# Norm blocks turned into a pair of score banks instead of two single banks

## The chip, the cores and the metric

The kernel runs on one core of one Trainium2 chip. The metric is the device time of one execution in microseconds (us); the unchanged kernel takes 1291.82 us, the median of three runs (1291.59 to 1291.99). The core has five instruction queues that run side by side and wait for each other through semaphores: TensorE (PE: matmuls and transposes), VectorE (DVE), ScalarE (ACT), GpSimd (POOL), and SyncE (SP), which issues the transfers. Results of matmuls and transposes land in PSUM, which the kernel lays out in banks of 128 partitions by 512 numbers of 32 bits.

## The reference

One layer of a decoder: 16 learned tokens are put ahead of 1024 input tokens (1040 in all, 1024 features), the sum is normalized, projected into seven parts, given to two kinds of heads (differential attention and a gated recurrence), projected back, and followed by a convolutional feed-forward part. Only the first step and the projection behind it matter here:

```python
h = jnp.concatenate([meta, x], axis=1)          # 1040 x 1024
a = rmsnorm(h, ln_mix_pre[l])                   # x * rsqrt(mean(x*x) + EPS) * gain
proj = a @ w_in[l]
dq, dk, dv, hq, hf, hi, hg = jnp.split(proj, SPLITS, axis=-1)
```

## The kernel before

**The first norm.** The tokens are taken in nine blocks of 128 (the last has 16), counted from 0 here; the third, fifth, seventh and ninth are blocks 2, 4, 6 and 8. For each block ACT squares the row with a running sum (`pre_stat`; its output `pj` is a throw-away tile in PSUM, the sum is `ss`) and makes 1/rms of it with a logarithm and an exponential. DVE multiplies the row by 1/rms and by the gain, in two halves of 512 features (`pre_scale`, output `xs`). PE turns each half into four 128x128 transposes (`pre_turn`, output `px`, line 292). ACT then copies the half rounded to a shorter format (`pre_hi`, a CAST, `a<-px`), and DVE subtracts this copy from the original for the remainder (`pre_lo`, a TENSOR_TENSOR, also `a<-px,a`). In the rows with numbers, `a00`, `a01`, `a02` are the rounded parts of three groups of tokens (0 to 255, 256 to 639, 640 to 1039), and `a10`, `a11`, `a12` their remainders.

**The projections beside it.** A projection of one column tile is three matmuls for each of eight feature blocks: rounded weights with rounded activations, rounded weights with the remainder, and remainder of the weights with rounded activations. Those of the first head of attention (`pi_dq`, `pi_dk`, `pi_dv` for query, key, value) run between the transposes of the norm blocks: the first group of tokens during blocks 2 to 4, the second during blocks 5 to 8. When a projection of a group is done, ACT and DVE take it out of PSUM (`q`, `k`, `kl` and `vt` in the rows), and its bank can be used again: `pi_dv` of the first group takes the bank of `pi_dq`. The weights `w3` of `pi_dv` are rounded on DVE (a CAST, `w<-wr_dv`) and their remainder is made on POOL.

**PSUM banks.** The pool has three kinds of tiles, each with two buffers: `ps_in` (one bank, projections), `ps_m` (one bank, everything small), and `ps_s` (a pair of banks, `[P, 2, 512]`, later the attention scores, in the norm the throw-away `pj`). A half block `px` takes a `ps_m` bank. Block 1 alone already takes one `ps_s` pair for both its halves (`spare`).

**What sets the order.** PE's order is written out: `interleave` runs the projections and the norm blocks as generators and mixes them by a cost budget. On ACT, DVE, POOL and SP a scheduler orders the instructions when the program is built, by its own estimates, and it puts in every semaphore wait. It keeps a record of who read and wrote each tile: a writer waits for the readers of what it overwrites, and a tile that gets a used buffer waits for the users of the tile before. Each engine runs its own list strictly in order, so that a wait holds everything behind it.

Of the kernel before, what the change touches and what calls it, by code (L numbers as in the profile page):

```python
# [90 lines left out]
def layer_kernel(ctx: ExitStack, tc: tile.TileContext, x, meta, table, lbl, gpre, gpost, win,  # L91
# [60 lines left out]
    def ps_m(name):  # L152
        return pp.tile([P, 512], F32, tag="m", name=name)

    def ps_s(name):
        return pp.tile([P, 2, 512], F32, tag="S", name=name)
# [115 lines left out]
    def pre_rows(i):  # L272
        return min(P, L - P * i)

    def pre_stat(i):
        r = pre_rows(i)
        junk = ps_s(f"pj{i}").rearrange("p a c -> p (a c)")
        ss = zp.tile([P, 1], F32, tag="ss", name=f"ss{i}", bufs=3)
        A.activation(junk[:r], xts[i][:r], AF.Square, accum_out=ss[:r])
        rstd_of(ss[:r], ss[:r], D)  # L280
        return ss

    def pre_scale(i, half, ss, xs):
        r = pre_rows(i)
        cs = slice(512 * half, 512 * half + 512)
        V.scalar_tensor_tensor(xs[:r, :512], xts[i][:r, cs], ss[:r], gb[:r, cs], ALU.mult, ALU.mult)

    def pre_turn(i, half, xs, pt=None):
        r = pre_rows(i)
        pt = ps_m(f"px{i}_{half}") if pt is None else pt  # L290
        for j in range(4):
            T.transpose(pt[:, j * r:(j + 1) * r], xs[:r, P * j: P * (j + 1)], ident[:r, :r])
        pv = pt[:, : 4 * r].rearrange("p (k t) -> p k t", k=4)
        return pv, slice(4 * half, 4 * half + 4), slice(P * i, P * i + r)

    def pre_hi(pv, ks, s):
        return A.copy(act(0, ks, s.start, s.stop), pv)

    def pre_lo(pv, ks, s):
        return V.tensor_tensor(act(1, ks, s.start, s.stop), pv, act(0, ks, s.start, s.stop).bitcast(F32), op=ALU.subtract)  # L300

    def pre_block(i):
        if i in stat:
            ss = stat[i]
        else:
            with tc.issue_after(last_hi.ins):
                ss = pre_stat(i)
        if i in xts:
            xs = zp.tile([P, D], F32, tag="xs", name=f"xs{i}")
            for half in range(2):  # L310
                pre_scale(i, half, ss, xs[:, 512 * half:])
            xts.pop(i)
        else:
            xs = xss[i, 0]
        for half in range(2):
            out_ = pre_turn(i, half, xs[:, 512 * half:])
            pre_hi(*out_)
            turned[i] = pre_lo(*out_)
            yield
# [614 lines left out]
    def pre_blocks(bs):  # L934
        for i in bs:
            yield from pre_block(i)
            if i + 4 < NBLK:
                load_x(i + 4)
# [865 lines left out]
```

## Time and profile before

| | |
|---|---|
| median of three runs | 1291.82 us |
| the profiled execution | 1290.12 us |
| its span, first to last instruction | 1288.3 us |
| PE busy in the span | 1268.2 us (98%) |
| DVE, ACT, POOL busy | 904.2, 692.1, 409.4 us |
| mean granted TensorE clock | 0.997 of full |
| the norm's transposes (`px`) | first at 7.8, last at 44.3 us from the start |

The profile is of one execution. A timeline row gives start and length in us, the engine, the line of the kernel, the operation, out<-in, the shapes and, after x, how many instructions were merged; in brackets stands how long the engine was idle just before and what ended it. L57 is the wrapper through which all DVE and ACT work goes, so these are told apart by their tiles. A window row gives for a stretch the busy time of each engine with its number of instructions, then the granted clock, the share of the DMA engines and GB/s. Matmuls overlap: a matmul's length is longer than the time until the next one starts.

### The profile page before, as it was taken

What the parts mean: (1) busy time and instruction counts of PE and PEld (TensorE: products, weight loads), DVE (VectorE), ACT (ScalarE), POOL (GpSimd) and SP (SyncE); (2) the same over time, 40 slices, a digit from 0 to 9 for tenths busy, and PEclk for the clock granted to TensorE, in tenths of its full rate; (3) what the DMA queues carried; (4) which work ended last, traced back from release to release, by engine and by line L of the source; (5) the groups of instructions that cost most, each with busy time, mean ns of one, the idle gap of its engine ahead of it and who ended that gap; (6) DMA issues with size and microseconds to landing.
All of it is one profiled execution on the core that took longest, in us unless ns stands there. A gap on an engine that the chain in (4) does not pass through costs nothing.

```text
span 1288.3 us, 26390 instructions
## 1 busy us (share of the span) xinstructions
PE 1268.2 (98%) x10264; PEld 1181.5 (92%) x10264; DVE 904.2 (70%) x1579; ACT 692.1 (54%) x1698; POOL 409.4 (32%) x322
## 2 busy tenths in 40 slices
PE   7999999999999999999999999999999999999997
PEld 7899999999999999777999999999999998888886
DVE  6576647564757476747797778778778786697587
ACT  7465357545654566446665445445445454454454
POOL 3221212021212110122165766766766730010120
PEclk9999999999999999999999999999999999999999
DMA  6222222212222223837512322222222237955363
GB/s 223 95 84 69 84 83 98 70 68 83 99 73 89 66 91 110 269 104 241 204 59 84 112 77 91 75 83 90 76 83 85 81 101 233 340 185 172 90 213 123
DMA packets 84387, 153.07 MB, mean 119 GB/s; under 512 B 9587, under 2 KB 19859, under 8 KB 84262
## 3 DMA queue, kind: packets, MB, share of 16 engines
q1 hardware_dynamic: 84262, 151.39, 35.4%
q8 instruction: 80, 1.31, 0.4%
q14 instruction: 45, 0.37, 0.1%
HBM read 112.69 MB, written 38.67 MB: 117 GB/s over the span
## 4 chain that ended last, share of the span: by engine, by line
PE 66%; DVE 2%; ACT 1%; DMA 0%; issue 0%; DVEq 0%
PE pd L1616 5%; PE pd L1615 5%; PE pd L1614 5%; PE pb L1415 4%; PE pb L1416 4%; PE pb L1417 4%; PE pa L1416 3%; PE pa L1417 3%; PE pa L1415 3%; PE pc L1416 3%; PE pc L1415 3%; PE pc L1417 3%; PE py L1030 2%; PE py L1034 2%; PE py L1032 2%; PE pq L1392 2%
## 5 line engine op out<-in xcount | busy, mean ns | idle before, releaser
L1415 PE MATMUL pb<-t,uh 128*128 128x258 f32 (+1 forms) x456 | 127.4, 279 | 0.6 <-DVE u L57 0.6
L1416 PE MATMUL pb<-t,uh 128*128 128x258 f32 (+1 forms) x456 | 127.3, 279 | 0.0
L1417 PE MATMUL pb<-t,ul 128*128 128x258 f32 (+1 forms) x456 | 127.2, 279 | 0.0
L1616 PE MATMUL pd<-wh,gl 128*128 128x512 f32 (+1 forms) x314 | 121.0, 386 | 0.0
L1615 PE MATMUL pd<-wl,gh 128*128 128x512 f32 (+1 forms) x314 | 120.5, 384 | 0.4 <-DVE wl L57 0.3
L1614 PE MATMUL pd<-wh,gh 128*128 128x512 f32 (+1 forms) x314 | 120.8, 385 | 0.0
L57 DVE SCALAR_TENSOR_TENSOR c<-uu,cwt,c 128x512 f32<-128x512 f32 x88 | 94.9, 1079 | 22.2 <-ACT c L57 21.4
L1364 POOL TENSOR_TENSOR c<-c,c 128x512 f32<-128x512 f32 x44 | 64.3, 1462 | 127.1 <-ACT c L57 112.9
L57 DVE SCALAR_TENSOR_TENSOR c<-ug,cwt,c 128x512 f32<-128x512 f32 x88 | 83.9, 954 | 6.6 <-ACT c L57 5.9
L1415 PEld LDWEIGHTS pb<-t,uh 128*128 128x128 f32 x456 | 85.8, 188 | 0.9 <-DVE u L57 0.8
L1416 PEld LDWEIGHTS pb<-t,uh 128*128 128x128 f32 x456 | 85.9, 188 | 0.0
L1417 PEld LDWEIGHTS pb<-t,ul 128*128 128x128 f32 x456 | 85.9, 188 | 0.0
L1416 PE MATMUL pa<-t,uh 128*128 128x256 f32 (+1 forms) x304 | 85.3, 281 | 0.0
L1417 PE MATMUL pa<-t,ul 128*128 128x256 f32 (+1 forms) x304 | 85.2, 280 | 0.0
L1415 PE MATMUL pa<-t,uh 128*128 128x256 f32 (+1 forms) x304 | 85.2, 280 | 0.0
L1417 PE MATMUL pc<-t,ul 128*128 128x256 f32 x304 | 83.9, 276 | 0.0
L1415 PE MATMUL pc<-t,uh 128*128 128x256 f32 x304 | 83.9, 276 | 0.0
L1416 PE MATMUL pc<-t,uh 128*128 128x256 f32 x304 | 83.9, 276 | 0.0
L1615 PEld LDWEIGHTS pd<-wl,gh 128*128 128x128 f32 x314 | 58.9, 188 | 14.0 <-DVE wl L57 1.5
L1616 PEld LDWEIGHTS pd<-wh,gl 128*128 128x128 f32 x314 | 59.0, 188 | 12.1
L1614 PEld LDWEIGHTS pd<-wh,gh 128*128 128x128 f32 x314 | 59.0, 188 | 11.6
L57 ACT ACTIVATE c<-ug,cbt,cwt 128x512 f32<-128x512 f32 x44 | 35.9, 817 | 44.0 <-issue 26.2
(421 smaller groups left out, 4278.2 us busy)
## 6 DMA issues: line engine op xcount, KB each, us to landing
ra<-in_wup_dram SPq DMA_DIRECT2D x76, 256.0 KB, 2.7
wd<-in_wdown_dram SPq DMA_DIRECT2D x44, 256.0 KB, 3.3
tsc<-wd SPq DMA_DIRECT2D x44, 256.0 KB, 2.5
gsc<-c SPq DMA_DIRECT2D x44, 256.0 KB, 2.0
wi<-tsc SPq DMA_DIRECT2D x44, 256.0 KB, 2.9
gi<-gsc SPq DMA_DIRECT2D x33, 256.0 KB, 4.0
wi<-in_wdown_dram SPq DMA_DIRECT2D x33, 256.0 KB, 3.7
msc<-mm SPq DMA_DIRECT2D x21, 256.0 KB, 3.6
```

The costliest lines, as they stand in the source:

```text
L57: ins = call(*args, **kw)
L1030: T.matmul(py[:r], mh[:, j, :r], hi, start=(first and j == 0), stop=False)
L1032: T.matmul(py[:r], mh[:, j, :r], lo, start=False, stop=False)
L1034: T.matmul(py[:r], ml[:, j, :r], hi, start=False, stop=(last and k == k1 - 1))
L1364: G.tensor_tensor(cg, cg, cu, op=ALU.mult)
L1392: T.matmul(pt, hi[:, s], th[:, k], start=(kh + k == 0), stop=False)
L1415: T.matmul(pt, hi[:, s], th[:, k], start=(first and k == 0), stop=False, skip_group_check=True)
L1416: T.matmul(pt, hi[:, s], tl[:, k], start=False, stop=False, skip_group_check=True)
L1417: T.matmul(pt, lo[:, s], th[:, k], start=False, stop=(k == 3), skip_group_check=True)
L1614: T.matmul(py, gh[:, s], wh, start=(k == 0 and pr not in (3, 7)), stop=False, skip_group_check=True)
L1615: T.matmul(py, gh[:, s], wl, start=False, stop=False, skip_group_check=True)
L1616: T.matmul(py, gl[:, s], wh, start=False, stop=(k == NH - 1), skip_group_check=True)
```

## The change

Blocks 2, 4, 6 and 8 take one `ps_s` pair for both halves, as block 1 does, instead of two `ps_m` banks. Blocks 3, 5 and 7 keep theirs. The number of operations, their shapes and PE's order stay the same.

```diff
         for half in range(2):
-            out_ = pre_turn(i, half, xs[:, 512 * half:])
+            if i % 2 == 0 and half == 0:
+                pair = ps_s(f"px{i}")
+            out_ = pre_turn(i, half, xs[:, 512 * half:], None if i % 2 else pair[:, half])
             pre_hi(*out_)
             turned[i] = pre_lo(*out_)
             yield
```

The rows below are the built programs' instructions in order, with the semaphores that each waits for. PE before, from the middle of the first group's projections: `px2_0` and `px2_1` are the two halves of block 2, `px3_0` the first half of block 3.

```order
L896 MATMUL pi_dk0_0_163<-a00_105,wl_dk0_1_272 128x256 [waits Pool_49]
L896 MATMUL pi_dk0_0_163<-a00_105,wl_dk0_1_272 128x256
L292 MATMUL px2_1_324<-ident_73,xs2_267 128x128 [waits DVE_49,PE_49]
L292 MATMUL px2_1_324<-ident_73,xs2_267 128x128 x3
L896 MATMUL pi_dk0_0_163<-a00_105,wl_dk0_1_272 128x256 x2
L896 MATMUL pi_dq0_0_162<-a10_106,wh_dq0_1_240 128x256 x4
L896 MATMUL pi_dk0_0_163<-a10_106,wh_dk0_1_271 128x256
L292 MATMUL px3_0_347<-ident_73,xs3_344 128x128 [waits DVE_49]
L292 MATMUL px3_0_347<-ident_73,xs3_344 128x128 x3
L896 MATMUL pi_dk0_0_163<-a10_106,wh_dk0_1_271 128x256 x3
L249 MATMUL pi_dv0_0_363<-a00_105,w30_281 128x256 [waits DVE_49,PE_49]
```

And PE with the change, where `px2` is the pair of block 2, and the row shown with it is the second half:

```order
L898 MATMUL pi_dk0_0_163<-a00_105,wl_dk0_1_272 128x256 [waits Pool_49]
L898 MATMUL pi_dk0_0_163<-a00_105,wl_dk0_1_272 128x256
L292 MATMUL px2_310<-ident_73,xs2_267 128x128 [waits DVE_49]
L292 MATMUL px2_310<-ident_73,xs2_267 128x128 x3
L898 MATMUL pi_dk0_0_163<-a00_105,wl_dk0_1_272 128x256 x2
L898 MATMUL pi_dq0_0_162<-a10_106,wh_dq0_1_240 128x256 x4
L898 MATMUL pi_dk0_0_163<-a10_106,wh_dk0_1_271 128x256
L292 MATMUL px3_0_346<-ident_73,xs3_343 128x128 x4
L898 MATMUL pi_dk0_0_163<-a10_106,wh_dk0_1_271 128x256 x3
L249 MATMUL pi_dv0_0_362<-a00_105,w30_281 128x256 [waits DVE_49,PE_49]
```

The second half of block 2 and the first half of block 3 have exchanged their waits. Before, `px2_1` waits for its input `xs2` and for an old bank; its count on DVE is that of the second half of `xs2`. `px3_0` gets the bank of `px2_0` and waits on DVE until that is free, which is after the subtraction `a11<-px2_0`. With the change `px3_0` has an old bank and no wait of its own, and the second half of `px2` waits on DVE for a higher count than before: the subtraction of the first half, which reads the same tile. The same holds for `px4`, `px6` and `px8`.

DVE before, from the first weights' rounding on:

```order
L57 CAST w30_281<-wr_dv0_0_235 128x512 [waits DMAHW4_49]
L57 SCALAR_TENSOR_TENSOR xs3_344<-xt3_219,ss3_276,gb_122 128x512
L57 CAST w31_282<-wr_dv0_1_244 128x512 [waits DMAHW5_49]
L57 TENSOR_TENSOR a11_109<-px2_0_310,a01_108 128x4x128 [waits Activation_49]
L57 TENSOR_TENSOR a11_109<-px2_1_324,a01_108 128x4x128 [waits Activation_49]
L57 SCALAR_TENSOR_TENSOR q0_0_133<-pi_dq0_0_162,q0_0_133 64x256 [waits PE_49,Activation_49]
L57 SCALAR_TENSOR_TENSOR q1_0_134<-pi_dq0_0_162,q1_0_134 64x256
L57 SCALAR_TENSOR_TENSOR xs4_389<-xt4_222,ss4_385,gb_122 128x512 [waits DMAHW3_49,DVE_49,Activation_49]
L57 TENSOR_TENSOR a11_109<-px3_0_347,a01_108 128x4x128 [waits Activation_49]
```

and with the change:

```order
L57 CAST w30_281<-wr_dv0_0_235 128x512 [waits DMAHW4_49]
L57 SCALAR_TENSOR_TENSOR xs3_343<-xt3_219,ss3_276,gb_122 128x512
L57 CAST w31_282<-wr_dv0_1_244 128x512 [waits DMAHW5_49]
L57 TENSOR_TENSOR a11_109<-px2_310,a01_108 128x4x128 [waits Activation_49]
L57 SCALAR_TENSOR_TENSOR xs4_388<-xt4_222,ss4_384,gb_122 128x512 [waits DVE_49,DMAHW3_49,PE_49,Activation_49]
L57 TENSOR_TENSOR a11_109<-px2_310,a01_108 128x4x128 [waits Activation_49]
L57 SCALAR_TENSOR_TENSOR xs4_388<-xt4_222,ss4_384,gb_122 128x512
L57 SCALAR_TENSOR_TENSOR q0_0_133<-pi_dq0_0_162,q0_0_133 64x256 [waits PE_49,Activation_49]
L57 SCALAR_TENSOR_TENSOR q1_0_134<-pi_dq0_0_162,q1_0_134 64x256
L57 TENSOR_TENSOR a11_109<-px3_0_346,a01_108 128x4x128 [waits Activation_49]
```

The list is the same up to the subtraction of block 2's first half. Behind it the scale `xs4` of block 4 has moved ahead of the second half's subtraction and of the query's two subtractions `q0`, `q1`, and its first row now waits for PE, since it overwrites `xs2` while the second half of `px2` still has to be turned.

ACT before, from the query's copies to the second half of block 4:

```order
L57 ACTIVATE q0_0_133<-pi_dq0_0_162 64x256 [waits PE_49]
L57 ACTIVATE q1_0_134<-pi_dq0_0_162 64x256
L57 ACTIVATE ss4_385<-ss4_385 128x1 [waits Activation_49]
L57 ACTIVATE pj5_459,ss5_460<-xt5_246 128x1024 [waits DMAHW6_49,DVE_49]
L57 CAST a01_108<-px3_0_347 128x4x128 [waits PE_49]
L57 CAST k0_0_135<-pi_dk0_0_163 64x256 [waits PE_49]
L57 CAST k0_0_135<-pi_dk0_0_163 64x256
L57 CAST k1_0_136<-pi_dk0_0_163 64x256 x2
L57 CAST a01_108<-px3_1_368 128x4x128 [waits PE_49]
L57 ACTIVATE ss5_460<-ss5_460,eps_78 128x1 [waits Activation_49]
L57 ACTIVATE pj6_506,ss6_507<-xt6_342 128x1024 [waits DMAHW7_49,DVE_49]
L57 CAST a01_108<-px4_0_392 128x4x128 [waits PE_49]
```

and with the change:

```order
L57 ACTIVATE q0_0_133<-pi_dq0_0_162 64x256 [waits PE_49]
L57 ACTIVATE q1_0_134<-pi_dq0_0_162 64x256
L57 CAST a01_108<-px3_0_346 128x4x128 [waits PE_49]
L57 CAST k0_0_135<-pi_dk0_0_163 64x256 [waits PE_49]
L57 CAST k0_0_135<-pi_dk0_0_163 64x256
L57 CAST k1_0_136<-pi_dk0_0_163 64x256 x2
L57 CAST a01_108<-px3_1_367 128x4x128 [waits PE_49]
L57 ACTIVATE pj5_457,ss5_458<-xt5_246 128x1024 [waits DMAHW6_49,DVE_49]
L57 CAST a01_108<-px4_391 128x4x128 [waits PE_49]
L57 ACTIVATE ss5_458<-ss5_458,eps_78 128x1 [waits Activation_49]
L57 ACTIVATE pj6_504,ss6_505<-xt6_341 128x1024 [waits DMAHW7_49]
L57 ACTIVATE ss5_458<-ss5_458 128x1 [waits Activation_49]
```

The sum `pj5` of block 5 has moved behind the key's copies and block 3, directly ahead of block 4's first half, and the copy of a second half now also waits for the subtraction of the first. Some way behind, `pj7` and `pj8` move in the same way, to either side of the first half of block 6. From the third group's projections on, all lists are the same.

## The prediction

> **What bounds the kernel now.** The page's first part and the window view first: where does PE, the busiest engine, stand still?
>
> ```profile
> PE 1268.2 (98%) x10264; PEld 1181.5 (92%) x10264; DVE 904.2 (70%) x1579; ACT 692.1 (54%) x1698; POOL 409.4 (32%) x322
> ...
> 48.00:200.00 152.00, 150.62 (x1392) 142.78 (x1392) 87.76 (x209) 81.14 (x241) 30.18 (x32) 1.00 0.28 89
> 200.00:600.00 400.00, 396.39 (x3734) 364.86 (x3733) 250.14 (x569) 221.04 (x656) 73.00 (x70) 1.00 0.33 109
> 600.00:1000.00 400.00, 398.69 (x3329) 393.10 (x3329) 316.53 (x412) 216.79 (x441) 238.02 (x163) 1.00 0.29 98
> 1000.00:1255.00 255.00, 254.73 (x1410) 220.94 (x1409) 192.46 (x290) 127.05 (x250) 52.06 (x37) 1.00 0.54 178
> ```
>
> PE is busy in 98% of the span. From 48 to 1255 us, stretches of 152 + 400 + 400 + 255 = 1207 us, it is busy for 150.62 + 396.39 + 398.69 + 254.73 = 1200.43, so it stands for 6.6 us, and its granted clock is 1.00. Whatever delays PE before 48 us has at most these 6.6 us to be made up in. The changed stage lies wholly before 48 us, so I read that stretch as a timeline, its first stall first.
>
> ```profile
> 17.08 0.63 PE L292 MATMUL px<-ident,xs 128*128 128x128 f32 x4
> ...
> 17.78 0.64 PE L896 MATMUL pi_dq<-a,wh_dq 128*128 128x256 f32 x4
> ...
> 18.25 0.28 PE L896 MATMUL pi_dk<-a,wh_dk 128*128 128x256 f32 x1
> ...
> 18.78 1.05 ACT L57 CAST a<-px 128x512 fp32r<-128x512 f32 x2
> ...
> 19.37 1.48 DVE L57 CAST w<-wr_dv 128x512 fp32r<-128x512 f32 x1
> ...
> 20.78 1.27 DVE L57 TENSOR_TENSOR a<-px,a 128x512 fp32r<-128x512 f32 x2
> ...
> 21.51 0.82 PE L292 MATMUL px<-ident,xs 128*128 128x128 f32 x4 [2.98 <-DVE a L57]
> ...
> 21.99 0.99 PE L896 MATMUL pi_dk<-a,wh_dk 128*128 128x256 f32 x3
> 22.07 0.86 DVE L57 SCALAR_TENSOR_TENSOR q<-pi_dq,q 64x256 fp32r<-64x256 f32 x2
> ...
> 23.07 0.55 PE L249 MATMUL pi_dv<-a,w 128*128 128x256 f32 x1
> ...
> 23.42 0.42 PE L251 MATMUL pi_dv<-a,w 128*128 128x256 f32 x1
> ...
> 23.64 0.41 PE L253 MATMUL pi_dv<-a,w 128*128 128x256 f32 x1
> ```
>
> The transposes at 17.08 are the second half of block 2, those at 21.51 the first half of block 3. Between them PE runs eleven issues, has nothing left at 18.25 + 0.28 = 18.53, and stands for 2.98 us, until DVE has subtracted block 2's first half. This subtraction is the first of the two at 20.78, so it ends at about 20.78 + 1.27/2 + 0.04 = 21.46. It is late for nothing that PE or ACT owes it: ACT's two copies are over at 18.78 + 1.05 = 19.83. It stands in DVE's list behind the rounding of the second value weights, which runs from 19.37 to 20.85.
>
> ```profile
> 21.00:22.00 1.00, 0.49 (x5) 0.49 (x5) 1.00 (x2) 0.95 (x2) 1.00 (x1) 0.93 0.92 311
> ...
> 22.00:25.00 3.00, 2.90 (x14) 2.64 (x13) 2.91 (x6) 2.05 (x5) 0.22 (x1) 0.50 0.32 78
> ...
> 25.00:26.00 1.00, 1.00 (x9) 1.00 (x9) 0.95 (x4) 0.84 (x3) 0.00 (x0) 0.86 0.00 0
> ```
>
> The clock column (0.93, 0.50 and 0.86; windows of two views, by start) says that behind the stall TensorE runs at half clock: 0.07 of a microsecond lost is 0.14 us at half, so from 21.86, and to 25.28. In it matmuls of this size start 0.22 us apart (23.42, 23.64); the four at 17.78 took 18.25 - 17.78 = 0.47 until the next, 0.12 each.
>
> **The change part by part.** No operation is added or removed; four second halves get a wait, the banks of `px3`, `px5`, `px7` come free earlier, and DVE and ACT are reordered. I go through PE's list and write how far it runs behind the kernel before.
>
> *Block 2.* The second half now waits for the subtraction that ends at 21.46. That one keeps its place in DVE's list, with the same work ahead, so PE goes on at 21.51 as before. But it stops at 17.08 and not at 18.53: 1.45 us of work that ran ahead of the stall now runs behind it, at half clock. Four transposes take 21.99 - 21.51 = 0.48, and seven matmuls 7 x 0.22 = 1.5. Block 3's first half, no longer waiting, starts at 23.5, or 2.0 late. What was removed (its wait) gains nothing, since the same subtraction now holds PE eleven issues earlier.
>
> The next rows are those of ACT, DVE and PE from which the next two steps are made (squares with their read-out, copies, one scale, one subtraction, block 3's second half and block 4's two):
>
> ```profile
> 17.72 1.03 ACT L57 ACTIVATE pj<-xt 128x1024 f32<-128x1024 f32 x1
> ...
> 18.69 0.19 ACT L57 ACTIVATION_READ_ACCUMULATOR pj<-xt 128x1 f32 x1
> ...
> 19.92 0.76 ACT L57 ACTIVATE q<-pi_dq 64x256 fp32r<-64x256 f32 x2
> ...
> 22.37 0.59 ACT L57 CAST a<-px 128x512 fp32r<-128x512 f32 x1 [0.42 <-PE px L292]
> ...
> 22.96 0.75 DVE L57 SCALAR_TENSOR_TENSOR xs<-xt,ss,gb 128x512 f32<-128x512 f32 x1
> 23.01 1.50 ACT L57 CAST k<-pi_dk 64x256 fp32r<-64x256 f32 x4
> ...
> 23.74 0.69 DVE L57 TENSOR_TENSOR a<-px,a 128x512 fp32r<-128x512 f32 x1
> ...
> 24.06 1.05 PE L292 MATMUL px<-ident,xs 128*128 128x128 f32 x4
> ...
> 25.92 0.60 PE L292 MATMUL px<-ident,xs 128*128 128x128 f32 x4
> ...
> 27.19 0.60 PE L292 MATMUL px<-ident,xs 128*128 128x128 f32 x4
> ```
>
> *The query's bank.* `pi_dv` needs the bank that DVE's two `q` subtractions free; before, these ended at 22.07 + 0.86 = 22.93 and PE followed 0.14 later, at 23.07. Now the last query matmul ends at about 23.5. ACT's two copies (0.76) end at 24.3. DVE, which runs `xs4`, the second half's subtraction and `xs4` again from 22.4 (0.75 + 0.69 + 0.75, each starting a little before the last ends), is free at about 24.45, so `q` ends at 25.3 and `pi_dv` starts at 25.4: 2.35 late. Now the clock pays back: the kernel before spends 23.07 to 25.28 at half clock, which costs it 1.1 us, while 25.4 lies behind the slow stretch. Four matmuls (0.47) bring block 3's second half to 25.9. From there to block 4 it is four transposes and seven matmuls, as from 25.92 to 27.19 before, 1.27 at full clock: block 4's first half at 27.15, only 1.2 late.
>
> *Block 4.* PE could turn the second half at 27.15 + 1.27 = 28.4, but now waits for the first half's subtraction. Ahead of that stand on ACT, in the new order: block 3's first copy after its transposes (23.5 + 1.05 = 24.55, so to 25.2), four key copies (1.50, to 26.7), block 3's second copy (0.59, to 27.3), the moved sum `pj5` (like the one at 17.72 with its read-out, 18.88 - 17.72 = 1.16, to 28.4), and block 4's copy (0.59, to 28.9). DVE's 0.69 ends at 29.6 and PE goes on at 29.65. That is a stall of 1.2 us where none was, and 29.65 - 27.19 = 2.45 late. This time hangs on ACT's chain, not on PE, so an error in the step before hardly moves it.
>
> ```profile
> 33.95 0.98 ACT L57 ACTIVATE q<-pi_dq 64x384 fp32r<-64x384 f32 x2
> ...
> 37.19 0.60 PE L292 MATMUL px<-ident,xs 128*128 128x128 f32 x4
> ...
> 43.89 0.66 PE L292 MATMUL px<-ident,xs 16*128 16x16 f32 x8
> 43.99 0.48 ACT L57 COPY vtva<-pi_dv 128x384 f32<-128x384 f32 x1 [1.18 <-PE pi_dv L253]
> 44.37 0.43 ACT L57 CAST a<-px 128x64 fp32r<-128x64 f32 x2
> 44.62 0.43 DVE L57 TENSOR_TENSOR a<-px,a 128x64 fp32r<-128x64 f32 x2 [1.07 <-ACT a L57]
> 44.90 0.91 PE L360 MATMUL pb<-oh,tbb 32*128 32x384 f32 x2 [0.35 <-DVE a L57]
> ```
>
> *Block 6.* Everything 2.45 late, ACT starts its `q` pair at 33.95 + 2.45 = 36.4 and ends it (0.98) at 37.4, the moved `pj7` (1.16) at 38.5, block 6's copy (0.59) at 39.1; DVE's subtraction (0.69) ends at 39.75. PE reaches the second half at 37.19 + 2.45 = 39.64: a stall of about 0.15, so 2.6 late. Below nothing this cannot go, since PE's own list is unchanged; above, 0.3 if ACT's rows don't overlap at all.
>
> *Block 8.* Before, its eight small transposes run on at 43.89, and the bias tables' first matmul waits 0.35 us, to 44.90. Now the second half has to wait for ACT's copy (half of 0.43, at 44.37 behind `vt`) and for DVE (half of 0.43): 44.62 + 0.22 + 0.05 = 44.89 before, 47.5 now. Its four transposes (a third of a microsecond at most) then still stand ahead of the tables' matmul: + 0.25. At 48 us PE is 2.45 + 0.15 + 0.25 = 2.85 late; I take **2.8**.
>
> *Behind 48 us.* Every list is as before, and I let the whole 2.8 through: what PE still waits for is fed by PE itself. Bounds: nothing made up, and 1.3 made up of the 6.6 us of standing (a fifth).
>
> The same sum with the clock otherwise: a slow stretch that ends earlier costs the changed kernel up to 0.4 less, since ACT's chain sets block 4; without the slow stretch in the kernel before, that one is 1.1 faster. Between 2.8 - 0.4 - 1.3 = 1.1 and 2.8 + 1.1 + 0.4 = 4.3, I keep 2.8, the case of the profile.
>
> [...]
>
> **The result.** The profiled execution before took 1290.12 us, with 1288.3 of span; after it that makes 1292.9. The median shown is 1.7 above that execution, so on the median: 1291.82 + 2.8 = **1294.6 us**, 0.22% slower. I count less than 0.2% (2.6 us) as no change.
>
> **The rivals.**
>
> *The clock.* If the timed runs of the kernel before mostly escape the slow stretch behind a 2.98 us stall, and those of the changed one don't behind 21.51 - 17.08 = 4.43, it is 2.8 + 1.1 = 3.9: 1295.7. For it speaks the longer stall; against it the narrow spread of the three runs (0.4 us), where a stretch that comes and goes would show 1.1.
>
> *Made up later (not slower).* Three of PE's waits behind 48 us, for work of DVE and ACT, make 2.9 us together (in all, times, longest):
>
> ```profile
> PE pi_dq L249 <- DVE gate L57: 1.1, 3, 0.4
> PE pn_vh L376 <- ACT pb L57: 1.0, 3, 0.4
> PE pl L492 <- DVE mix L57: 0.8, 3, 0.3
> ```
>
> If DVE and ACT kept their times there while PE comes late, these waits would shrink: it decides from 2.8 of the 6.6 us on, and the time is 1291.8. Half of it gives 1293.2, no change either. Against it: these waits end with work on PE's own results, which come later too.
>
> [...]
>
> **How the numbers follow.** The forecast (2.0 to 3.3 late) has 0.5, the clock 0.2, made up in part or whole 0.2, the freed PE 0.05; 0.05 stays for what I don't see. Slower by over 0.2% takes two thirds of the forecast, nearly all of the clock's and 0.03 of the rest: 0.55. Faster gets 0.03, for no case ends there; within 0.2% is 0.42. The range goes from 1.1 to 4.3: 1292.9 to 1296.1.
>
> **What would show it.** Right: PE's last issue ahead of the first stall is the key's pair at about 16.8, that stall is 4.4 us long and released by DVE's `a`; a second stall of about 1.2 us at 28 to 30, released by DVE's `a` behind a `pj` on ACT; the tables' first matmul at 47.7; and from 48 us on PE's standing still 6 to 7 us. Wrong: the first stall still begins at 18.5 (the pair does not wait), the subtraction of block 2's first half ends elsewhere than at 21.5, or the tables' matmul is 2.8 late and the last output is not.

## The result

The changed kernel takes 1296.3 us, the median of 8 executions (1294.2 to 1301.06); the kernel before, run beside it, takes 1291.3 (8 executions, 1290.38 to 1292.82). The ratio is 1.0041, 95% interval 1.0032 to 1.0049, so the change costs 5.0 us by the medians, 5.3 (4.1 to 6.3) by the ratio. When it was run once more for the last experiment the ratio was 1.0031 (1.0019 to 1.0043), 3.7 us between the medians. The forecast was 1294.6 us: 2.8 above the 1291.82 of the first three executions of before, of which eight now give 1291.3. It was right in its sign and too small in size.

The profiled execution of the change has a span of 1294.7 us, 6.4 above the 1288.3 of the one before. Its timeline through the changed stage (lines behind 315 are two higher than before):

```profile
17.19 0.60 PE L292 MATMUL px<-ident,xs 128*128 128x128 f32 x4
...
18.21 0.39 PE L898 MATMUL pi_dk<-a,wl_dk 128*128 128x256 f32 x2
...
21.69 0.66 PE L292 MATMUL px<-ident,xs 128*128 128x128 f32 x4 [3.10 <-DVE a L57]
...
23.07 1.05 PE L292 MATMUL px<-ident,xs 128*128 128x128 f32 x4
...
24.49 0.86 DVE L57 SCALAR_TENSOR_TENSOR q<-pi_dq,q 64x256 fp32r<-64x256 f32 x2
...
25.49 0.55 PE L249 MATMUL pi_dv<-a,w 128*128 128x256 f32 x1 [0.72 <-DVE q L57]
...
28.06 1.03 ACT L57 ACTIVATE pj<-xt 128x1024 f32<-128x1024 f32 x1
...
28.83 1.04 PE L292 MATMUL px<-ident,xs 128*128 128x128 f32 x4
...
29.91 0.59 ACT L57 CAST a<-px 128x512 fp32r<-128x512 f32 x1 [0.70 <-PE px L292]
...
30.53 0.69 DVE L57 TENSOR_TENSOR a<-px,a 128x512 fp32r<-128x512 f32 x1 [1.64 <-ACT a L57]
...
31.27 0.66 PE L292 MATMUL px<-ident,xs 128*128 128x128 f32 x4 [0.58 <-DVE a L57]
...
49.36 0.41 PE L292 MATMUL px<-ident,xs 16*128 16x16 f32 x4 [0.60 <-DVE a L57]
49.63 0.89 PE L362 MATMUL pb<-oh,tbb 32*128 32x384 f32 x2
```

The stops are where the prediction put them, in PE's order. PE's last pair ahead of the first stop is the key's (18.21), and it then stands 3.10 us for DVE at block 2's second half (21.69). `pi_dv` follows 0.72 us late behind the query's subtraction (24.49 + 0.86 = 25.35). Block 4's second half (31.27) waits 0.58 us for a subtraction (30.53) that follows ACT's copy (29.91). ACT's square `pj5` (28.06) is no longer what holds that copy up: it is read out by 29.2, and ACT then stands 0.70 us for PE's transposes of the first half (28.83 to 29.87). Block 8's second half (49.36, 16 rows) waits 0.60 us, and the tables' first matmul comes behind it, at 49.63.

What the prediction did not have is in the clock. In the window rows the engines come in the order PE, its weight loads, DVE, ACT, POOL; the number behind them is the granted clock:

```profile
23.00:26.00 3.00, 2.28 (x11) 2.01 (x10) 2.93 (x6) 2.50 (x7) 0.00 (x0) 0.50 0.18 42
26.00:29.00 3.00, 3.00 (x16) 3.00 (x15) 1.61 (x4) 1.74 (x3) 0.00 (x0) 0.50 0.36 89
29.00:30.00 1.00, 1.00 (x8) 1.00 (x7) 0.00 (x0) 0.30 (x3) 0.00 (x0) 0.63 0.90 233
...
48.00:200.00 152.00, 150.02 (x1388) 141.28 (x1387) 87.70 (x213) 78.55 (x235) 30.42 (x33) 1.00 0.27 88
200.00:600.00 400.00, 395.11 (x3730) 364.59 (x3730) 247.83 (x571) 220.77 (x655) 68.45 (x67) 1.00 0.32 105
600.00:1000.00 400.00, 398.94 (x3305) 391.61 (x3305) 316.21 (x409) 217.04 (x444) 241.09 (x162) 1.00 0.31 101
1000.00:1255.00 255.00, 254.74 (x1434) 221.97 (x1433) 191.79 (x289) 126.13 (x245) 52.53 (x36) 1.00 0.53 177
```

From 23 to 29 us and into the thirtieth the clock is 0.50: the granted-clock record starts at 22.91 and ends at 29.73, 6.83 us or two windows of 3.41, where the kernel before had one (21.87 to 25.28). A window at 0.50 costs, by estimate, 3.41 x 0.50 = 1.7 us of PE's work, if PE has work. `pi_dv`, which starts at 25.49, runs at half clock until 29.73 (its products start 0.21 us apart at 28.19, 28.40 and 28.61, and 0.12 at 29.95 and 30.07), where the forecast had it at full speed from its first product.

Behind 48 us nothing is made up: PE stands for 1.98 + 4.89 + 1.06 + 0.26 = 8.2 us there, against 6.6 before. The 1.6 us more are no effect of the change, as far as can be seen: the lists are the same from there on, and in the profiles of the eleven edited kernels below PE's standing there lies between 0.3 us under and 2.1 us over that of before. The profiled execution of before was a short one (1290.12 us against a median of 1291.09 in the 94 that were run beside the experiments). Profiles are therefore read below for where PE stands, and the medians for how much it costs.

### The profile page after: what moved, and what is told of

Its sections match the earlier page's. It is cut to its first block, busy times and chain, and to the rows that moved or that the text cites. A ratio compares the mean times of both kernels' runs of the same rounds, so it can differ in the third digit from the quotient of the medians.

```text
span 1294.7 us, 26387 instructions
## 1 busy us (share of the span) xinstructions
PE 1270.8 (98%) x10264; PEld 1182.6 (91%) x10264; DVE 906.1 (70%) x1579; ACT 692.9 (54%) x1698; POOL 411.1 (32%) x322
## 4 chain that ended last, share of the span: by engine, by line
PE 62%; DVE 4%; ACT 2%; issue 1%; DMA 0%; DVEq 0%; SPq 0%; ACTq 0%
PE pd L1617 5%; PE pd L1618 5%; PE pd L1616 5%; PE pb L1417 4%; PE pb L1418 4%; PE pb L1419 4%; PE pa L1418 3%; PE pa L1417 3%; PE pa L1419 3%; PE pc L1418 3%; PE pc L1419 3%; PE pc L1417 3%; PE pq L1394 2%; PE pq L1396 2%; PE pq L1395 2%; PE py L1032 1%
## 5 line engine op out<-in xcount | busy, mean ns | idle before, releaser
L1241 POOL TENSOR_TENSOR ws<-ra,ra 128x512 f32<-128x512 f32 x38 | 56.8, 1495 | 8.5 <-DMA ra<-in_wup_dram 5.8
```

The lines of the kernel that those rows point to most:

```text
L1241: G.tensor_tensor(sums[nm], a, b, op=op)
```

## Clock and stops apart

Each execution lists its span and its mean granted clock. One less the clock, times the span, is the time lost to the clock in that execution; taking it from the execution's time leaves the rest. A clock in three digits is good to 0.6 us in one execution, so only means are used. About 1.2 us of the loss (mean of 14 profiles) belongs to the last microseconds of the program, where PE has little to do, and is common to all. The split is bookkeeping: time at half clock in which PE stands counts as lost to the clock (0.72 of the 6.83 us in the profile of the change), so the two parts are not two separate causes. The last two columns show the difference from the kernel before, over those 94 executions (mean time 1291.25, clock 2.58 with a standard error of 0.10, rest 1288.67). A standard error stands behind each clock mean. The kernels are those of the experiments below.

| kernel | executions | median, us | ratio to before, 95% interval | lost to the clock, us | clock, over before | rest, over before |
|---|---|---|---|---|---|---|
| the change, both times together | 14 | 1295.8 | 1.0041 (1.0032 to 1.0049); 1.0031 (1.0019 to 1.0043) | 4.07 (0.51) | +1.5 | +3.2 |
| only_px2 (pair in block 2 alone) | 11 | 1293.6 | 1.0021 (1.0012 to 1.0030) | 3.76 (0.44) | +1.2 | +1.4 |
| only_px4 (block 4 alone) | 11 | 1292.1 | 1.0008 (0.9999 to 1.0017) | 3.05 (0.31) | +0.5 | +0.4 |
| only_px6_8 (blocks 6 and 8 alone) | 11 | 1292.4 | 1.0010 (1.0001 to 1.0018) | 3.05 (0.50) | +0.5 | +0.8 |
| lone_half (pairs, halves in tiles of their own) | 11 | 1292.4 | 1.0008 (0.9999 to 1.0017) | 3.64 (0.34) | +1.1 | +0.1 |
| q_first (scalings behind the query) | 8 | 1294.6 | 1.0024 (1.0014 to 1.0034) | 3.23 (0.42) | +0.7 | +2.7 |
| fill_q (stop at `pi_dv` filled) | 7 | 1294.9 | 1.0028 (1.0017 to 1.0039) | 3.70 (0.87) | +1.1 | +2.5 |
| fill_stop (first stop filled) | 9 | 1294.4 | 1.0023 (1.0013 to 1.0032) | 2.01 (0.31) | -0.6 | +3.9 |
| sub_first (subtraction ahead of the CAST) | 11 | 1293.4 | 1.0020 (1.0011 to 1.0029) | 2.47 (0.41) | -0.1 | +2.5 |
| sub_q_first (both moves on DVE) | 11 | 1292.4 | 1.0008 (0.9999 to 1.0017) | 2.70 (0.37) | +0.1 | +1.3 |
| before_sub_first (the same move in the kernel before) | 11 | 1290.9 | 0.9998 (0.9989 to 1.0007) | 2.46 (0.32) | -0.1 | -0.4 |
| before_pool_cast (before, CAST on POOL) | 11 | 1289.65 | 0.9990 (0.9981 to 0.9999) | 1.87 (0.27) | -0.7 | -0.8 |

In the mean the change costs 4.7 us: 3.2 of the rest, which holds the stops (standard error 0.4), and 1.5 of clock (0.5).

## The experiments

Two theories stood against each other at first. *Stalls alone* is the prediction: the second halves wait, the clock is that of before. *Two windows*: the stop of 0.7 us at `pi_dv` keeps the clock at half speed for a second window.

### One block at a time

```diff
-            if i % 2 == 0 and half == 0:
+            if i in (2,) and half == 0:
                 pair = ps_s(f"px{i}")
-            out_ = pre_turn(i, half, xs[:, 512 * half:], None if i % 2 else pair[:, half])
+            out_ = pre_turn(i, half, xs[:, 512 * half:], pair[:, half] if i in (2,) else None)
```

and the same with `(4,)` and with `(6, 8)`.

> Only block 2 is turned into a pair; blocks 4, 6 and 8 keep two single banks. Theory of the prediction (stalls alone; the clock is at half speed for one window of 3.4 us, as before): PE stops ahead of px2's second half, is about 2 us late behind it and 1.2 us late at px4, so the time is 1.0 to 1.5 us above before. Rival, two slow windows (the short stop of PE at pi_dv for the query's subtraction, 0.7 us in the profile of the change, keeps the clock at half speed for a second window, half of 3.4 us = 1.7 us): 2.9 to 3.6 us above before, with half clock over some 6.8 us in the profile.

> Only block 4 is turned into a pair. Stalls alone: the first 25 us are those of before, one slow window, and px4's second half waits for the first half's subtraction behind ACT's order: 1.2 us (prediction) above before; by the profile of the change (0.6 us of waiting there) 0.5 to 0.8 us. Two slow windows: the same, since block 2 is where the second one comes from; 0.5 to 1.2 us. If this alone comes to 2.5 us or more, block 4 is the main cause and both are wrong.

> Only blocks 6 and 8 are turned into pairs; 2 and 4 as before. Stalls alone: 0.15 us at px6's second half and 0.25 us at px8's (0.6 us there in place of the 0.35 us that pb waited for): 0.3 to 0.5 us above before. With the clock: px8's two halves of 16 rows, the stop of 0.6 us between them and the first product of the tables (32 rows) stand together for 2.2 us; in 3 of 8 profiles of pairs so far a window that holds them all was followed by one at half speed (1.7 us). One time in three gives 0.6 us more: 0.8 to 1.2 us above before. Together with the measured 2.6 us of block 2 alone and 1.1 us of block 4 alone the whole change (5.0 us) leaves 1.3 us for this pair of blocks if the parts simply add.

Block 2 alone: ratio 1.0021, 2.7 us (1.5 to 3.9), between the two theories and nearer to the second. Its profile, timeline and windows:

```profile
21.23 0.66 PE L292 MATMUL px<-ident,xs 128*128 128x128 f32 x4 [2.89 <-DVE a L57]
...
25.03 0.55 PE L249 MATMUL pi_dv<-a,w 128*128 128x256 f32 x1 [0.54 <-DVE q L57]
```

```profile
22.00:25.00 3.00, 2.49 (x14) 2.20 (x13) 2.92 (x6) 2.31 (x6) 0.00 (x0) 0.54 0.23 68
...
26.00:29.00 3.00, 3.00 (x16) 3.00 (x15) 1.94 (x4) 2.13 (x7) 0.00 (x0) 0.50 0.55 113
```

The stop at `pi_dv` is 0.54 us, and the clock is still 0.50 at 29 us: two windows. Block 4 alone costs 1.0 us (-0.1 to 2.2), blocks 6 and 8 together 1.3 (0.1 to 2.3). 2.7 + 1.0 + 1.3 = 5.0: the parts add up to the whole (each is known to about 1.1 us), and block 2 is the largest. One part of what was expected fell. The kernel with block 4 alone has block 2 as before, and its profile shows two windows all the same (PE stands 3.07 and then 0.55 us for `q`). So the second window is no mark of the change in block 2. That the change makes such windows more frequent is read from the mean loss in the table above, not from the profiles.

### The shared tile

```diff
-            out_ = pre_turn(i, half, xs[:, 512 * half:], None if i % 2 else pair[:, half])
+            out_ = pre_turn(i, half, xs[:, 512 * half:], None if i % 2 or half else pair[:, 0])
```

> Each even block's first half goes into one bank of a score pair, its second half into a single bank as before, so that no second half shares a tile with a first half. If the wait of the second half for the first half's subtraction is the root (prediction, and also the two slow windows that follow from it): within 1 us of before, PE stops ahead of px3's first half or later, one slow window. If the root is the use of the score pairs as such (the squares pj and the turns sharing them, ACT's order): 3 to 5 us above before, as with the change.

```profile
24.03 0.36 PE L249 MATMUL pi_dv<-a,w 128*128 128x256 f32 x1 [3.43 <-DVE q L57]
```

1.0 us above before (-0.1 to 2.2), with 0.1 us of it in the rest and all the remainder in the clock. With the halves in tiles of their own, PE ran past block 3's first half and stopped at `pi_dv`, for 3.43 us. ACT still squares `pj5` directly ahead of block 4's first half, as with the change, so the pairs as such and that order on ACT add next to nothing to the rest (0.1 us, standard error 0.4). On DVE block 4's scalings stand behind the query's subtraction again, as before. So the root of the stops is the second half's wait on the shared tile, together with the order on DVE that comes with it; the next run parts the two. The 1.1 us of clock (standard error 0.3) go with one stop of 3.43 us where before has 2.98.

### The query's subtraction ahead of the scalings

```diff
-                pre_scale(i, half, ss, xs[:, 512 * half:])
+                with tc.issue_after(q_last[0].ins) if i == 4 else nullcontext():
+                    pre_scale(i, half, ss, xs[:, 512 * half:])
...
```

(`q_last` holds the second subtraction of `q`; the two lines that set it are left out.)

> The change, with block 4's scalings (xs, DVE) held behind the query's subtraction. It takes away PE's stop of 0.7 us at pi_dv. Stalls alone: 0.6 us is gained, of which the later stops give some back: 4.3 to 4.8 us above before. Two slow windows: the second window goes too, 1.7 us more: 2.3 to 3.2 us above before, with half clock over one window of 3.4 us in the profile. If scaling px4 late costs a new stop at px4's first half, it is seen there and added.

3.1 us (1.8 to 4.4) by the ratio, inside what two windows expected, though the medians lie 3.6 us apart. The profile shows what was to go: no stop at `pi_dv`, and one window at half speed, 22.20 to 25.61. The order on DVE is thus a small part of the rest (2.7 us, standard error 0.5, against the change's 3.2), and the wait on the shared tile most of it. The profile also shows 0.82 us of standing at block 4's second half (0.58 and 0.83 in the two profiles of the change), and a new window at half speed where nobody looked for one, at 49.5 us:

```profile
46.47 0.41 PE L292 MATMUL px<-ident,xs 16*128 16x16 f32 x4
47.48 0.41 PE L292 MATMUL px<-ident,xs 16*128 16x16 f32 x4 [0.60 <-DVE a L57]
47.75 0.89 PE L363 MATMUL pb<-oh,tbb 32*128 32x384 f32 x2
```

```profile
45.00:49.00 4.00, 3.40 (x21) 2.51 (x20) 2.75 (x12) 1.30 (x5) 0.00 (x0) 1.00 0.00 0
49.00:50.00 1.00, 1.00 (x7) 0.99 (x6) 0.68 (x2) 0.00 (x0) 0.21 (x1) 0.75 0.00 0
50.00:53.00 3.00, 3.00 (x12) 2.89 (x11) 0.00 (x0) 1.20 (x3) 0.00 (x0) 0.51 0.28 84
```

PE stands for only 0.60 us ahead of it. But from 46.47 to the end of the tables' first matmul at about 48.57, some 2.1 us, PE has nothing but two small turns (16 rows), the stop, and a matmul of 32 rows.

### Filling PE's stops

Products of zeros (`az[1]` is a tile of zeros) go into PE's queue ahead of the waiting instruction; no other engine's list moves, save that with sixteen of them one load on SP moves behind three others. The table `early` hands the filled bank on to block 3; the second form shows only the lines that differ from the first.

```diff
-    spare = {}
+    spare, early = {}, {}
...
+        early[3, 1] = ps_m("px3_1")
+        for _ in range(3):
+            T.matmul(early[3, 1][:, :P], az[1], az[1], start=True, stop=True)
         yield from proj_group(0, parts[2], tiles[2][1], tiles[2][2])
...
-            out_ = pre_turn(i, half, xs[:, 512 * half:], None if i % 2 else pair[:, half])
+            out_ = pre_turn(i, half, xs[:, 512 * half:], early.pop((i, half), None) if i % 2 else pair[:, half])
```

> The change, with three products of zeros (128x128, f32, into the bank that px3's second half writes afterwards) in PE's queue ahead of pi_dv. They fill PE's stop of 0.7 us there and move no instruction of another engine. Two slow windows (a window in which the clock is at half speed and PE stops for more than some 0.5 us keeps it there): half clock for 3.4 us instead of 6.8 in the profile and PE up to 1.7 us earlier, of which px4's second half gives back some, since its subtraction waits behind ACT's square pj5: 3.3 to 4.1 us above before. Stalls alone: nothing is gained, 4.9 to 5.3 us above before.

```diff
+            if (i, half) == (2, 1):
+                early[3, 0] = ps_m("px3_0")
+                for _ in range(16):
+                    T.matmul(early[3, 0][:, :P], az[1], az[1], start=True, stop=True)
...
```

> The change, with sixteen products of zeros in PE's queue ahead of px2's second half, in the stop of 3.1 us. If the stop is what lowers the clock, the clock is full in the profile at 22 to 26 us; PE then reaches pi_dv earlier and waits there for the query's subtraction (DVE, 24.5 to 25.4 us) about 2 us, and goes on from 25.3 at full clock: 3 to 4.3 us above before; if that second stop lowers the clock in its turn, 4.5 to 5.5 us. If the clock falls all the same in the window behind the filled stop, activity of PE does not set it.

With three, the profile has one window at half speed (21.14 to 24.56) and none behind, and the time is 3.6 us above before (2.2 to 5.0), as two windows expected. The interval also reaches the other theory, so the time does not decide, and the profile of one execution does not either, since the change itself came out without a second window in another (below).

With sixteen the clock behind the filled stop is full:

```profile
20.00:22.00 2.00, 2.00 (x20) 2.00 (x20) 1.40 (x2) 0.00 (x0) 1.64 (x2) 1.00 0.73 227
22.00:25.00 3.00, 2.14 (x19) 1.94 (x17) 2.34 (x4) 2.27 (x6) 0.16 (x1) 1.00 0.41 111
```

```profile
25.68 0.36 PE L249 MATMUL pi_dv<-a,w 128*128 128x256 f32 x1 [1.53 <-DVE q L57]
```

With the stop filled, the clock no longer falls at 22 us. This profile alone would not show that PE's activity sets it, by the same reason as above; the nine executions do: their loss to the clock is 2.0 us (standard error 0.3), half of the change's 4.1 (0.5). Still the kernel is 3.0 us (1.7 to 4.1) slower than before. PE went on without a stop and stood 1.53 us for `q` at `pi_dv` (25.68; 25.49 in the change), since DVE sets that time. Of the 2.1 us of clock that the filling takes away, the mean time gains 1.4; the rest reads 3.9 where it was 3.2, a difference of one and a half standard errors. So it is not shown that all of what the split calls clock can be won back.

### The subtraction ahead of the second CAST

The subtraction that every form of the kernel waits for stands on DVE behind the rounding of the second value weights. The split of those weights moves behind it:

```diff
-    for c in range(2):
+    def third_split(c, ins):
         raw = raws[2, c]
-        with tc.issue_after(V.last.ins):
+        with tc.issue_after(ins):
...
+    third_split(0, V.last.ins)
...
             turned[i] = pre_lo(*out_)
+            if i == 2 and half == 0:
+                third_split(1, turned[i].ins)
```

> The change, with DVE's subtraction for px2's first half ahead of the second CAST w<-wr_dv instead of behind it. PE's stop at px2's second half ends 1.4 us earlier and is some 1.6 us long. If the clock falls as before, the gain is that 1.4 us: 3.4 to 3.9 us above before; if a stop of 1.6 us is too short to lower it, both slow windows go as well: 0.5 to 2 us above before. If the second CAST becomes late for pi_dv instead, nothing is gained and a new stop stands there.

> The kernel before, with the same move: the subtraction for px2's first half ahead of the second CAST. PE's stop at px3's first half ends 1.4 us earlier: 1.2 to 1.5 us below before if the clock falls all the same, 2.5 to 3.3 us below if it doesn't; no gain if q's subtraction, 2 us behind it on DVE, is what PE then waits for at pi_dv.

```profile
20.40 0.66 PE L292 MATMUL px<-ident,xs 128*128 128x128 f32 x4 [1.98 <-DVE a L57]
...
24.64 0.36 PE L249 MATMUL pi_dv<-a,w 128*128 128x256 f32 x1 [1.96 <-DVE q L57]
```

```profile
22.00:25.00 3.00, 1.04 (x9) 0.87 (x8) 2.92 (x5) 2.51 (x7) 1.05 (x1) 1.00 0.36 118
...
26.00:29.00 3.00, 3.00 (x16) 3.00 (x16) 0.71 (x2) 2.27 (x5) 0.00 (x0) 0.52 0.55 130
```

In the change, PE goes on at 20.40 instead of 21.69 and then stands 1.96 us at `pi_dv`: the CAST, moved down, now stands ahead of `q` together with the scalings. 2.6 us above before (1.4 to 3.7): a gain of 2 us on the change, less than expected if no window falls. In this profile the second stop is long enough to lower the clock (1.00 up to 25 us, 0.52 from 26 to 29). In the mean, though, the clock costs no more than in the kernel before (-0.1), and the whole 2.5 us stand in the rest: two stops of some 2 us in place of 3.10 and 0.72. In the kernel before, the same move gains nothing that can be told (0.9998, 0.9989 to 1.0007): its stop at block 3 shrinks to 0.16 us, and a stop of 1.38 us for `q` takes its place. The third case of its expectation came in: PE waits for `q` instead.

> The change with both moves on DVE: px2's first subtraction ahead of the second CAST, and block 4's scalings behind the query's subtraction. Of the two stops that the run with the first move alone showed (1.98 us at px2's second half, 1.96 us at pi_dv) the second shrinks to 0.4 us or so, and no window of PE up to 28 us then stands for more than 1.8 us, which in no profile so far lowered the clock: 0.8 to 1.8 us above before. If the scalings, now late, hold up px4 (0.8 us in the run that moved them alone), 1.6 to 2.4 us.

```profile
22.00:25.00 3.00, 2.07 (x18) 1.90 (x18) 2.74 (x7) 2.72 (x7) 0.30 (x1) 1.00 0.63 163
```

Both moves together bring the change to 1.0 us above before (-0.1 to 2.2), inside 0.8 to 1.8. Its stops are 1.50, 0.93 (0.4 was expected) and 0.84 us, no window falls in the profile, and the loss to the clock is that of before (2.70 against 2.58). Most of what the pairs cost is thus a matter of what stands ahead of two subtractions in DVE's list. The kernel before was not run with both moves, so how much they would gain there is open.

### A CAST on POOL

```diff
-        with tc.issue_after(V.last.ins):
-            V.tensor_copy(third[c][:, 0], raw)
+        with tc.issue_after(V.last.ins) if c == 0 else nullcontext():
+            (G if c else V).tensor_copy(third[c][:, 0], raw)
```

> The kernel before, with the second CAST w<-wr_dv on POOL instead of DVE (behind POOL's own part of the first piece; the split computes the same). DVE goes from block 3's scaling to the two subtractions of px2 and to q's 1.4 us earlier: PE's stop at px3's first half ends at about 20.1 us instead of 21.5 and q is no longer late for pi_dv, so no window falls to half speed: 2 to 3.2 us below before. If POOL is too slow, pi_dv waits for the second weight piece at its fifth block of rows (23 us) and the gain is 0 to 1 us; 1.3 us lost if POOL needs over 2.5 us for the CAST.

```profile
18.48 0.43 DVE L57 CAST w<-wr_dv 128x512 fp32r<-128x512 f32 x1
...
19.54 1.29 DVE L57 TENSOR_TENSOR a<-px,a 128x512 fp32r<-128x512 f32 x2
...
20.29 0.66 PE L292 MATMUL px<-ident,xs 128*128 128x128 f32 x4 [0.79 <-DVE a L57]
20.66 0.61 POOL L923 CAST w<-wr_dv 128x512 fp32r<-128x512 f32 x1
20.87 0.86 DVE L57 SCALAR_TENSOR_TENSOR q<-pi_dq,q 64x256 fp32r<-64x256 f32 x2
...
21.76 2.09 DVE L57 SCALAR_TENSOR_TENSOR xs<-xt,ss,gb 128x512 f32<-128x512 f32 x2
...
21.87 0.36 PE L249 MATMUL pi_dv<-a,w 128*128 128x256 f32 x1 [0.58 <-DVE q L57]
...
24.63 0.66 PE L292 MATMUL px<-ident,xs 128*128 128x128 f32 x4 [0.78 <-DVE a L57]
```

The scheduler also moved block 4's second scaling ahead of block 3's first subtraction, and one square on ACT and one load on SP have other places. POOL needs 0.61 us for the CAST (20.66). DVE goes from the first CAST over one scaling to both subtractions (19.54), PE stands 0.79, 0.58 and 0.78 us instead of 2.98 in one piece, and no window falls in this profile. The kernel takes 0.9990 of before (0.9981 to 0.9999, so just clear of no change), 1.3 us less, or 1289.65 against 1291.27 in the medians. That is less than the 2 to 3.2 us expected; the two later stops were not in the sum.

### The change once more

> The change itself once more, unedited, for the one quantity that is still rough: how much of its loss is clock. From the eight executions so far, the time lost to the clock (one less the granted clock, by the span) is 4.5 us with a standard error of 0.8, against 2.6 to 2.8 us of before in 84 executions. If the clock is a cause of its own, these come out at 3.7 to 4.8 us again, the time at 4.3 to 5.3 us above before, and the profile shows at least two windows at half speed ahead of 60 us. If the prediction's size was right and the eight were unlucky, the loss to the clock is 2.5 to 3.2 us and the time 2.8 to 3.6 us above before.

3.7 us between the medians, 3.45 us (standard error 0.55) lost to the clock: between the two expectations, and the mean over both times, 4.07, is 1.5 above before. The six new executions alone are 0.9 above it, which would not settle the clock's part by itself. The expected two windows were not in this profile. There was none:

```profile
17.93 0.39 PE L898 MATMUL pi_dk<-a,wl_dk 128*128 128x256 f32 x2
...
21.48 0.66 PE L292 MATMUL px<-ident,xs 128*128 128x128 f32 x4 [3.17 <-DVE a L57]
...
25.28 0.36 PE L249 MATMUL pi_dv<-a,w 128*128 128x256 f32 x1 [1.53 <-DVE q L57]
...
27.10 0.60 PE L292 MATMUL px<-ident,xs 128*128 128x128 f32 x4
...
28.01 0.57 ACT L57 CAST a<-px 128x512 fp32r<-128x512 f32 x1
...
29.36 0.66 PE L292 MATMUL px<-ident,xs 128*128 128x128 f32 x4 [0.83 <-DVE a L57]
...
47.45 0.41 PE L292 MATMUL px<-ident,xs 16*128 16x16 f32 x4 [0.60 <-DVE a L57]
47.72 0.89 PE L362 MATMUL pb<-oh,tbb 32*128 32x384 f32 x2
```

```profile
20.00:22.00 2.00, 0.52 (x5) 0.52 (x6) 1.43 (x2) 0.00 (x0) 1.64 (x2) 1.00 0.82 260
22.00:25.00 3.00, 1.75 (x16) 1.55 (x14) 2.72 (x5) 2.64 (x7) 0.19 (x1) 1.00 0.26 84
25.00:26.00 1.00, 0.72 (x6) 0.75 (x7) 0.97 (x3) 0.65 (x2) 0.00 (x0) 1.00 0.25 66
26.00:29.00 3.00, 2.53 (x22) 2.32 (x20) 1.69 (x4) 2.53 (x6) 0.00 (x0) 1.00 0.46 87
```

The same list with a stop of the same length (3.17 us against 3.10), and the clock is 1.00 throughout. What differs is where the windows lie. The clock's records in this profile put their borders at 13.29 and every 3.41 us from there, so at 16.70, 20.12 and 23.53: the stop, from 18.32 to 21.48, is cut into 1.80 and 1.36 us. In the profile of the change they lie at 19.49 and 22.91, and 2.20 us of the stop fall into one window. Here block 4's copy on ACT (28.01) does follow `pj5` without a pause, as forecast.

## What lowers the clock, and what keeps it low

Doing this for all 14 profiles (borders from the granted-clock records, PE's standing from its timeline) shows one pattern without exception for the windows between 10 and 43 us:

| clock in a window of 3.41 us | PE stands in it, us | clock in the next window |
|---|---|---|
| 1.00 | 0 to 1.80 (the largest: 1.53, 1.58, 1.76, 1.80) | 1.00 |
| 1.00 | 1.96, 2.20, 2.38, 2.41, 2.48, 2.68, 2.98, 3.19 | 0.50 |
| 0.50 | 0 to 0.50 (0.10, 0.14, 0.50) | 1.00 |
| 0.50 | 0.54, 0.55, 0.72 | 0.50 |

In these profiles the clock fell behind 1.96 us of standing in a window and more, and not behind 1.80 and less; it came back behind 0.50 us and less, and not behind 0.54 and more. The expectation of the run with both moves on DVE used the 1.8 us ahead of time, and no window fell there. The windows are those of the records: they last 10.24, 3.41 and 1259.52 us in the profile of before and 10.24, 6.83 and 1262.93 in that of the change, which is 3, 1 and 369, and 3, 2 and 370 times 3.4133 (a fourth, at the program's end, is no whole number of them), and the slow ones start 21.87 and 22.91 us from the start of the program. If the borders fall at random, a stop of 3.1 us escapes when they cut it into two pieces below 1.9 us each, in (2 x 1.9 - 3.1) / 3.41, or about a fifth, of the executions; this is an estimate from the table. No whole window of standing was needed: the 2.98 us stop in the profile of before, shorter than 3.41 us, lowered the clock, and so did one of 1.96. The table is what 14 profiles have in common, and says nothing of kernels whose PE work is of other kinds.

The window at 49.5 us fits if the small turns and the 32-row matmul count as standing. In the four profiles in which one window holds the whole of the 2.1 us (q_first, fill_stop, sub_first, only_px6_8) the standing counted so is 2.03 us, and the next window was at half speed. In the four others with the pair in block 8 a border cuts it, and it was not; counted so, no window that kept the clock has more than 1.80 us in any of the 14 profiles up to 55 us. The turns of 128 rows do not fit as standing: with them, a window of 2.34 us kept the clock and one of 2.09 lowered it. That is argued from where the borders fell; no run changed the size of those matmuls.

## Why the prediction was right or wrong

| step of the prediction | forecast, us | the change | once more |
|---|---|---|---|
| *Block 2*: length of the first stop | 4.4 | 3.10 | 3.17 |
| *Block 2*: block 3's first half starts | 23.5 | 23.07 | 22.80 |
| *The query's bank*: `pi_dv` starts | 25.4 | 25.49 | 25.28 |
| block 4's first half, after "the clock pays back" | 27.15 | 28.83 | 27.10 |
| *Block 4*: second half starts; its stop | 29.65; 1.2 | 31.27; 0.58 | 29.36; 0.83 |
| *Block 8*: the tables' first matmul | 47.7 | 49.63 | 47.72 |

**Right.** The second half waits for DVE's subtraction of the first, that subtraction keeps its time, and `pi_dv` is late through `q` behind `xs4`. In the execution in which no window fell, block 4's second half hangs on ACT's order with `pj5`, and the starts from `pi_dv` to the tables' matmul come out within 0.3 us of the forecast. That the last of them meets it so closely (47.72 against 47.7) is luck: block 4's second half came 0.3 us earlier than forecast, and blocks 6 and 8 lost 0.25 more. Taking the shared tile away took the cost in the rest away (lone_half). Nothing was made up behind 48 us in the profiles, so that rival fell. No run shows the freed PE that has 0.05 in the chances: block 2's second half waited 3.10 and 3.17 us for the subtraction.

**Wrong, and the step that failed.** It is the step "Now the clock pays back" of *The query's bank*: `pi_dv` at 25.4 was put behind the slow stretch, because that stretch was taken from the profile of before with its place and length. In the profile of the change the stretch went on to 29.73, since PE stood 0.72 us at `pi_dv` inside its first window. The step was to bring block 4's first half to 27.15; it came at 28.83. The shelter behind it, *Block 4*'s "an error in the step before hardly moves it", failed with it: ACT stood 0.70 us for these late transposes, and the second half came 1.6 us late (31.27 against 29.65). The cases of the sum had a slow stretch that ends earlier and one that is missing before, but none that goes on for a second window: the clock's difference between the kernels stood at nothing. In the mean over executions it is 1.5 us (standard error 0.5), most of what the forecast lacks.

The rival *The clock* had this sign and nearly this size (3.9 us). It had before escape its slow stretch and the change not. Measured, it is a matter of how often: without the 1.2 us at the program's end, before loses 1.4 us, 0.8 of a window of 1.7, and the change 2.9, or 1.7 windows. Of the 94 executions of before 26 list a clock of 0.999 or more, too high for a whole window beside the program's end; of the 14 of the change one does, that of its second profile.

**Sizes.** The first stop was forecast from block 2's first half at 15.72 us in the profile of before. In none of the 13 other profiles is it that early (16.41 to 17.61, the change 17.19 and 16.91), in kernels with the same PE list up to there, so 4.4 us became 3.1. It did no harm to the sum, since the stop ends with DVE and not with its start. *Block 4*'s stop was 0.6 to 0.8 us instead of 1.2; in the execution with full clock it ended at nearly the forecast time (29.36). *Block 8* was put at 0.25 us as turns ahead of the matmul; in fact its second half stands 0.60 us where `pb` stood 0.35, which is that 0.25, and besides, in four of the eight profiles with the pair in block 8 the window behind the jam was at half speed. Blocks 6 and 8 alone measured 1.3 us (0.1 to 2.3), where 0.4 was in the sum. The stops of the whole change are 3.2 us in the mean (standard error 0.4) against the 2.8 forecast, so they agree; with the clock's 1.5 that is 4.7.

## What to carry to other kernels

When a queue runs ahead into a known stall, sharing a tile between two steps that used to be independent moves the stall earlier, and the work that ran ahead of it comes behind it. Price a stall not by its length alone but by how it can fall into the clock's windows: here a stop of 3.10 us lowered the clock to 0.50 and one of 3.17 left it at 1.00, by where the borders lay, and a second stop behind it (0.72 us, in other profiles 0.54 and 0.55) kept it at 0.50 for another window. A stage's clock in one profile is one draw; before building a sum on it, look at the clock of several executions.

## What was not expected of the hardware

A stop shorter than a window lowered the clock, and a much shorter one kept it low: 1.96 us of standing in 3.41 was followed by 0.50, and so was 0.54 us in a window that was at 0.50 already (the table above).

Some of DVE's operations took longer while POOL worked, and others did not. The first CAST `w<-wr_dv` took 0.42 us in the profile of the change and the second, of the same size, 1.49, while POOL split the first piece (in the kernel before: 1.48 against 0.42). In the kernel with the CAST on POOL, the two scalings at 21.76 took 2.09 us, by estimate about 1.4 for the first of them, beside POOL's split (21.34 to 22.63), as one takes 0.75 with POOL idle (22.96 in the profile of before); the two subtractions at 19.54, which read PSUM and also ran beside POOL, took 1.29 for both, where one takes 0.69 with POOL idle (23.74 in the profile of before). What in the operations makes this difference no run shows. So here DVE was the dear place for the second CAST (1.48 us), and POOL the cheap one (0.61).
